# Projection weights on GpSimd's transfer queue, and four buffers for the last output tiles

## The chip, the cores and the metric

The kernel runs on one core of a Trainium2 chip. The metric is the device time of one execution in microseconds (us). TensorE (PE) does the matrix products, VectorE (DVE) and ScalarE (ACT) the elementwise work, GpSimd (POOL) a few small operations, and SyncE (SP) issues transfers.

## The reference

Two layers of a hybrid trunk, for 256 context and 512 latent tokens with 1024 channels, all in float32. In each layer one wide projection feeds three head groups, whose gated outputs are joined, projected back and added to the residual under a layer norm:

```python
h_l = x * (1 + sc_l) + sh_l
parts_l = jnp.split(h_l @ w_in, in_splits(), axis=-1)      # the same for the context, h_c
ssd_l, ssd_c = ssd_mixer(parts_c[0:3], parts_l[0:3], ...)
mla_l, mla_c = mla_mixer(parts_c[3:7], parts_l[3:7], ...)
ret_l, ret_c = retention_mixer(parts_c[7:11], parts_l[7:11], ...)
out_l = jnp.concatenate([ssd_l, mla_l, ret_l], -1) @ w_out
x_new = layer_norm(ALPHA * x + g_l * out_l, ln_g, ln_b)    # the result of layer 2 is the output
```

The modulations sh, sc and g of every layer come from products of a conditioning vector with `w_ada`.

## The kernel before, in words

**Tiling.** Activations lie channel-major, as tiles of 128 channels x 768 tokens (columns 0 to 255 context, 256 to 767 latent). Each weight matrix is cut into tiles of 128 partitions x 1024 columns (512 KB). A layer has 42 such tiles of `w_in` and 16 of `w_out`, so 116 in all.

**A weight tile's way** is `wslot` (L153). A transfer fills a raw buffer `wr` (two of them); ACT rounds it into `wh` (L122), and DVE takes the rest, `wl = wr - wh` (L124 through L104); `wh` and `wl` have three buffers each. A matrix product is then three passes (L145): high by high, high by low, low by high. A raw buffer is free again when `wl` has been made, and a `wh` when the products of the tile before it in that buffer are done. From the seventh tile on, `wslot` runs at high priority.

**Stages of a layer.** `dt_stage`, `xbc`, `ssd` and the spilled projections (the list STEPS, L48); `zstage` and `ret`; `mla_prep`; then `mla` with the first half of the output projection beside it (`out_s`, L1147, tiles `sh`, `sl`); and the second half with the layer norm (`out_m`, L1167, and `lns`, L1203, tiles `mr`, `mh`). Intermediate results are spilled to DRAM and loaded again, all through `load` (L97), which issues on SyncE's queue: `cf<-cum`, `kr<-kn`, `mraw<-m`, `la<-a` are such loads. Layer 1 of the trace ends near 850 us, where the first projections of the second layer (`proj_lat`, L194) begin.

**Order.** The kernel gives program order and priorities; the program builder makes from these, when the kernel is built, one fixed order of instructions per engine and per queue, and the waits between them. SyncE and GpSimd work their own lists off strictly in order: what waits holds up what is behind it.

**GpSimd's list** is short. It has the zeroing of `rh` in `ret` (L805), memsets of the attention's operand tiles in `mla` (L999 to L1002, tiles `bql`, `bkh`, `bkl`, `bvh`), the sums `lxs` over the first tiles in `lns` (L1232), and `rp_y`, a power of -0.5 of the variance in `rpow` (L142) that each layer norm needs before it can go on.

**The end.** `ln_turned` (L1265) writes the last 256 tokens token-major: it holds four accumulators `pot`, adds the mean's part to each by a product (L1289), scales each on DVE into a tile `ho` of 128 x 512 with two buffers (L1290, L1291), and stores it (L1292). Nothing comes after these stores.

Of the kernel before, what the change touches and what calls it, by code (L numbers as in the profile page):

```python
# [9 lines left out]
F32 = mybir.dt.float32  # L10
# [78 lines left out]
class Trunk:  # L89
# [63 lines left out]
    def wslot(self, src, n=1024):  # L153
        self.nslots += 1
        with (self.tc.high_priority() if self.nslots > 6 else ExitStack()):
            raw = self.wp.tile([128, 1024], F32, tag="wr", name="wr", bufs=2)
            self.load(raw[:, :n], src)
            hi = self.wp.tile([128, 1024], F32R, tag="wh", name="wh", bufs=3)
            lo = self.wp.tile([128, 1024], F32R, tag="wl", name="wl", bufs=3)
            self.split(hi[:, :n], lo[:, :n], raw[:, :n])  # L160
        return hi, lo
# [1103 lines left out]
    def ln_turned(self, P, X, a, b, qsum, xsum):  # L1265


        pc = self.pc[self.l]
        k = (b - a) // 128
        dg, lgr, lbr = self.turn  # L1270
        po = {}
        for f in range(2):
            for c in range(k):
                po[c, f] = (self.acc.tile([128, 512], F32, tag="acc", name="pot") if f or c else
                            self.ps("pot", "pot", 1))
                for t in range(4):
                    self.mm(po[c, f][:, t * 128:(t + 1) * 128], X[4 * f + t][:, c * 128:(c + 1) * 128], dg[:, 4 * f + t],
                            t == 0, False, skip_group_check=True)
        with self.tc.high_priority():
            pd = self.ps("plm", "pld", 2)  # L1280
            self.mm(pd[0:1, 0:b - a], self.selD[:, 0:1], xsum)
            nd = P.tile([1, 256], F32, name="nd")
            self.act(nd[:, 0:b - a], pd[0:1, 0:b - a], AF.Copy, scale=-1.0)
            v = self.variance(P, qsum, xsum, k)
            y = self.rpow(P, v, k)
        for f in range(2):
            fs = slice(512 * f, 512 * f + 512)
            for c in range(k):
                self.mm(po[c, f], nd[:, c * 128:(c + 1) * 128], lgr[:, fs], False, True, skip_group_check=True)  # L1289
                o = P.tile([128, 512], F32, tag="hr", name="ho", bufs=2)  # L1290
                self.stt(o, po[c, f], y[:, c:c + 1], lbr[:, fs], ALU.mult, ALU.add)  # L1291
                self.load(self.out[1][c * 128:(c + 1) * 128, fs], o)  # L1292

# [145 lines left out]
```

## Time and profile before

| | |
|---|---|
| median of 3 runs | 1485.49 us (1483.68 to 1488.11) |
| profiled execution, device time | 1483.76 us |
| its span, first to last instruction | 1481.8 us |
| TensorE busy | 1426.5 us, 96% of the span |
| VectorE, ScalarE, GpSimd busy | 73%, 47%, 2% |
| transfers | 226.18 MB, nearly all on one hardware queue |

The span leaves some 2.0 us of the device time around it. A busy TensorE in this profile is one with a product in its pipeline. A matrix product and the weight load for the next one overlap, so PE and PEld together are more than the span.

### The profile page before, as it was taken

What the parts mean: (1) busy time and instruction counts of PE and PEld (TensorE: products, weight loads), DVE (VectorE), ACT (ScalarE), POOL (GpSimd) and SP (SyncE); (2) the same over time, 40 slices, a digit from 0 to 9 for tenths busy, and PEclk for the clock granted to TensorE, in tenths of its full rate; (3) what the DMA queues carried; (4) which work ended last, traced back from release to release, by engine and by line L of the source; (5) the groups of instructions that cost most, each with busy time, mean ns of one, the idle gap of its engine ahead of it and who ended that gap; (6) DMA issues with size and microseconds to landing.
All of it is one profiled execution on the core that took longest, in us unless ns stands there. A gap on an engine that the chain in (4) does not pass through costs nothing. (4 is left out here: it accounts for less than half of the span.)

```text
span 1481.8 us, 23394 instructions
## 1 busy us (share of the span) xinstructions
PE 1426.5 (96%) x8696; PEld 1158.2 (78%) x8696; DVE 1076.6 (73%) x2077; ACT 692.6 (47%) x1377; POOL 25.7 (2%) x35
## 2 busy tenths in 40 slices
PE   6999999999999999999999899999999999989988
PEld 4787789778888888777788778788778887767667
DVE  3599894995486667678645858997776767678846
ACT  2346743662232443477622345565463344347742
POOL 0000000000000001000001000000000000100010
PEclk9999999999999999999999999999999999999999
DMA  8336553457725746624241223353357465562241
GB/s 337 138 99 180 183 168 110 158 184 256 258 72 175 247 154 198 222 82 131 80 170 58 91 88 111 120 148 114 98 168 251 136 199 190 171 205 89 69 141 57
DMA packets 109725, 226.18 MB, mean 153 GB/s; under 512 B 13534, under 2 KB 41310, under 8 KB 109356
## 3 DMA queue, kind: packets, MB, share of 16 engines
q1 hardware_dynamic: 109612, 224.70, 46.5%
q8 instruction: 68, 1.11, 0.3%
q14 instruction: 45, 0.37, 0.1%
HBM read 174.46 MB, written 50.20 MB: 152 GB/s over the span
## 5 line engine op out<-in xcount | busy, mean ns | idle before, releaser
L101 PE MATMUL pj<-hh,wh 128*128 128x512 f32 (+1 forms) x984 | 354.5, 361 | 2.8 <-ACT hh L115 2.4
L101 PE MATMUL pj<-hh,wl 128*128 128x512 f32 (+1 forms) x984 | 353.2, 359 | 0.0
L101 PE MATMUL pj<-hl,wh 128*128 128x512 f32 (+1 forms) x984 | 350.7, 356 | 0.0
L122 ACT CAST wh<-wr 128x1024 fp32r<-128x1024 f32 (+1 forms) x116 | 120.3, 1039 | 208.8 <-PE pj L101 92.2
L101 PEld LDWEIGHTS pj<-hh,wh 128*128 128x128 f32 x984 | 185.1, 188 | 36.0 <-issue 8.9
L101 PEld LDWEIGHTS pj<-hh,wl 128*128 128x128 f32 x984 | 185.0, 188 | 31.2 <-issue 7.0
L101 PEld LDWEIGHTS pj<-hl,wh 128*128 128x128 f32 x984 | 185.2, 188 | 30.5 <-issue 6.4
L104 DVE TENSOR_TENSOR wl<-wr,wh 128x1024 fp32r<-128x1024 f32 (+1 forms) x116 | 141.0, 1216 | 79.6 <-ACT wh L122 78.5
L104 DVE TENSOR_TENSOR pel<-pe,peh 128x512 fp32r<-128x512 f32 (+1 forms) x112 | 71.6, 648 | 37.0 <-ACT peh L115 36.5
L107 DVE SCALAR_TENSOR_TENSOR cv<-xpad,cw,cv 128x772 f32<-128x772 f32 (+1 forms) x96 | 92.2, 993 | 0.2
L115 ACT ACTIVATE pe<-psc 128x512 f32<-128x512 f32 (+1 forms) x112 | 63.7, 569 | 56.4 <-PE psc L101 47.6
L1043 DVE TENSOR_REDUCE nm<-pmx 128x1 fp32r<-128x768 f32 (+1 forms) x80 | 67.6, 845 | 15.7 <-PE pmx L101 14.5
L101 PE MATMUL po<-sh,wh 128*128 128x512 f32 (+1 forms) x192 | 70.0, 367 | 4.2 <-DVE oy L107 4.2
L101 PE MATMUL po<-sl,wh 128*128 128x512 f32 (+1 forms) x192 | 70.1, 366 | 1.9 <-DVE sl L107 1.9
L115 ACT ACTIVATE ce<-cf 64x512 f32<-64x512 f32 (+1 forms) x80 | 46.9, 587 | 50.3 <-DMA cf<-cum 49.5
L101 PE MATMUL po<-sh,wl 128*128 128x512 f32 (+1 forms) x192 | 69.6, 364 | 0.0
L115 ACT ACTIVATE tm<-sf,dt 128x128 f32<-128x128 f32 x160 | 52.5, 390 | 30.4 <-DVE sf L104 30.3
L115 ACT ACTIVATE peh<-psc 128x512 fp32r<-128x512 f32 (+1 forms) x112 | 63.6, 568 | 0.2
L101 PE MATMUL po<-mr,wh 128*128 128x256 f32 (+1 forms) x216 | 55.5, 343 | 3.1 <-DVE la L107 3.1
L115 ACT ACTIVATE arg<-arg,ncb 128x128 f32<-128x128 f32 x160 | 54.9, 393 | 4.1 <-DVE arg L107 3.6
L101 PE MATMUL pv<-wl,hh 128*128 128x256 f32 x192 | 54.0, 281 | 0.7 <-DVE wl L104 0.7
L101 PE MATMUL pv<-wh,hh 128*128 128x256 f32 x192 | 53.7, 280 | 0.0
(337 smaller groups left out, 2952.1 us busy)
## 6 DMA issues: line engine op xcount, KB each, us to landing
wr<-in_win SPq DMA_DIRECT2D x82, 512.0 KB, 3.8
ar<-in_wada SPq DMA_DIRECT2D x48, 512.0 KB, 7.0
cf<-cum SPq DMA_DIRECT2D x80, 256.0 KB, 4.6
wr<-in_wout SPq DMA_DIRECT2D x32, 512.0 KB, 4.3
y<-ys SPq DMA_DIRECT2D x20, 256.0 KB, 2.5
xs<-th SPq DMA_DIRECT2D x16, 256.0 KB, 2.1
x<-in_xT SPq DMA_DIRECT2D x8, 384.0 KB, 8.6
rv<-stv SPq DMA_DIRECT2D x24, 128.0 KB, 3.0
```

Source lines behind the costliest of these rows:

```text
L101: return self.nc.tensor.matmul(out, lhsT=lhsT, rhs=rhs, start=start, stop=stop, **k)
L104: return self.nc.vector.tensor_tensor(out, a, b, op=op)
L107: return self.nc.vector.scalar_tensor_tensor(out, in0=a, scalar=s, in1=b, op0=op0, op1=op1)
L115: return self.nc.scalar.activation(out, in_, f, **k)
L122: self.nc.scalar.copy(hi, raw)
L1043: nc.vector.tensor_reduce(nm[:, i:i + 1], p1[:, 0:n], axis=AX.X, op=ALU.max, negate=True)
```

## The change

From the fourth weight tile on, `wslot` issues its transfer from GpSimd's queue; the first three stay on SyncE's, as do all other transfers. The last output tiles `ho` get a tag of their own with four buffers in place of the two of tag `hr`.

```diff
@@ wslot
         self.nslots += 1
         with (self.tc.high_priority() if self.nslots > 6 else ExitStack()):
             raw = self.wp.tile([128, 1024], F32, tag="wr", name="wr", bufs=2)
-            self.load(raw[:, :n], src)
+            (self.nc.gpsimd if self.nslots > 3 else self.nc.sync).dma_start(out=raw[:, :n], in_=src)
             hi = self.wp.tile([128, 1024], F32R, tag="wh", name="wh", bufs=3)
@@ ln_turned
                 self.mm(po[c, f], nd[:, c * 128:(c + 1) * 128], lgr[:, fs], False, True, skip_group_check=True)
-                o = P.tile([128, 512], F32, tag="hr", name="ho", bufs=2)
+                o = P.tile([128, 512], F32, tag="ho", name="ho", bufs=4)
                 self.stt(o, po[c, f], y[:, c:c + 1], lbr[:, fs], ALU.mult, ALU.add)
                 self.load(self.out[1][c * 128:(c + 1) * 128, fs], o)
```

## Rows read from the trace of the kernel before

**Rows 1.** The page: busy us by engine; the chain that ended last, by engine.

```profile
PE 1426.5 (96%) x8696; PEld 1158.2 (78%) x8696; DVE 1076.6 (73%) x2077; ACT 692.6 (47%) x1377; POOL 25.7 (2%) x35
...
PE 31%; DVE 5%; DMA 3%; ACT 3%; issue 1%; SPq 0%; POOL 0%; DVEq 0%; ACTq 0%; POOLq 0%
```

**Rows 2.** Waits of PE: us in total, times, longest.

```profile
PE pr L101 <- DMA ar<-in_wada: 7.5, 2, 6.6
...
PE pv L101 <- DVE wl L104: 0.7, 1, 0.7
...
PE pj L101 <- ACT wh L122: 0.4, 1, 0.4
```

**Rows 3.** Tile wr: ns min/median/max; then what its users waited for (us, times).

```profile
L104 DVE TENSOR_TENSOR wl<-wr,wh x116: 551/1224/1487, 14.6 to 1449.3; 128x1024 fp32r<-128x1024 f32 x114, 128x384 fp32r<-128x384 f32 x2
L98 SPq DMA_DIRECT2D wr<-in_win x84: 327/333/1122, 4.5 to 1192.8; - x84
...
  PE pj L101: 92.2, 43
...
  DMA wr<-in_win: 3.7, 3
  DMA wr<-in_wout: 2.7, 1
...
DMA to landing us min/median/max: 3.2/3.9/9.2
```

**Rows 4.** Waits of SyncE's queue, the longest group.

```profile
SPq L98 <- DVE wl L104: 240.3, 67, 11.8
```

**Rows 5.** SyncE's timeline, 1293 to 1312: start, us, transfer.

```profile
1298.06 0.38 SPq L98 DMA_DIRECT2D qr<-qh  x1
1301.71 0.33 SPq L98 DMA_DIRECT2D wr<-in_wout  x1
1302.14 0.47 SPq L98 DMA_DIRECT2D kr<-kn  x1
```

**Rows 6.** PE's timeline in that stretch.

```profile
1303.27 0.79 PE L101 MATMUL po<-sh,wh 128*128 128x512 f32 x1 [3.69 <-DVE oy L107]
```

**Rows 7.** Windows: length, busy us of PE, PEld, DVE, ACT, POOL; granted clock; DMA share, GB/s.

```profile
592.70:629.80 37.10, 34.40 (x199) 26.69 (x198) 25.12 (x36) 18.27 (x33) 0.00 (x0) 0.91 0.67 222
815.00:852.00 37.00, 31.18 (x174) 26.65 (x173) 32.09 (x64) 12.37 (x19) 1.73 (x2) 0.91 0.25 91
1296.60:1333.60 37.00, 32.20 (x130) 23.44 (x129) 29.39 (x44) 17.29 (x28) 0.00 (x0) 0.91 0.68 205
```

**Rows 8.** DVE's timeline at the end, and SyncE's stores.

```profile
1474.28 1.54 DVE L107 SCALAR_TENSOR_TENSOR ho<-pot,rp_y,lbr 128x512 f32<-128x512 f32 x2 [1.08 <-PE pot L101]
1477.15 1.56 DVE L107 SCALAR_TENSOR_TENSOR ho<-pot,rp_y,lbr 128x512 f32<-128x512 f32 x2 [1.33 <-DMA out<-ho]
...
1475.06 4.01 SPq L98 DMA_DIRECT2D out<-ho  x4
```

**Rows 9.** POOL's timeline: start, us, operation, idle before.

```profile
794.76 0.74 POOL L1232 TENSOR_TENSOR lxs<-lxs,la 128x256 f32<-128x256 f32 x1 [1.18 <-DVE la L107]
829.83 1.03 POOL L142 TENSOR_TENSOR rp_y<-rvv,mhalf 128x4 f32<-128x4 f32 x1 [34.33 <-DVE rvv L104]
...
1293.60 0.74 POOL L1000 MEMSET bkh<- 1x768 f32 x1 [8.58 <-PE pq L101]
...
1443.16 2.28 POOL L1232 TENSOR_TENSOR lxs<-lxs,la 128x512 f32<-128x512 f32 x1 [0.90 <-DVE la L107]
```

**Rows 10.** SyncE's weight transfers at the end of the first layer.

```profile
796.61 8.97 SPq L98 DMA_DIRECT2D wr<-in_win  x2
...
829.27 0.33 SPq L98 DMA_DIRECT2D wr<-in_win  x1
...
831.85 0.33 SPq L98 DMA_DIRECT2D wr<-in_win  x1
```

**Rows 11.** PE's timeline there.

```profile
830.92 0.82 PE L101 MATMUL prs<-K,rp_y 128*128 128x128 f32 x5 [0.81 <-POOL rp_y L142]
```

**Rows 12.** DVE's timeline, a weight split beside POOL's sum.

```profile
786.75 1.49 DVE L104 TENSOR_TENSOR wl<-wr,wh 128x1024 fp32r<-128x1024 f32 x1 [0.48 <-ACT wh L122]
```

## The prediction

> **What bounds the kernel now.** I read the page's engine line first: TensorE is busy 96% of the span, so 1481.8 - 1426.5 = 55.3 us of idle time is nearly all that a better supply could win back [rows 1]. Then the waits of PE, to see who causes that idle time. The largest that names a transfer is 7.5 us at the very start, for the modulation weights, which the change leaves alone; waits for a weight tile's halves `wh` and `wl` come to 1.1 us over 116 tiles [rows 2]. The view of tile `wr` says why: its ACT and DVE users waited for a transfer four times, 6.4 us in all, but 92.2 us for products that still held a `wh` buffer [rows 3]. So weights wait for TensorE, not TensorE for weights. Last, SyncE's own waits: it stood 240.3 us, 67 times, at the head of its list for `wl`, that is, with a weight transfer whose raw buffer was not yet free [rows 4]. That is what the change removes from SyncE, and the question is who stood behind.
>
> **Weight transfers, moved.** 116 - 3 = 113 of them leave SyncE. Issuing one takes 0.33 us there [rows 3], 37 us in all, on a sequencer that is not on the chain of work (SPq 0%) [rows 1]: worth nothing by itself. On GpSimd no row shows what an issue costs. From below it is SyncE's 0.33 us [rows 3], from above the longest operation that GpSimd runs here, 2.28 us [rows 9]; I take 1.03 us, the time of `rp_y` with its four columns, since that is an instruction with hardly any data, as an issue is [rows 9]. The landing, 3.9 us at the median [rows 3], then comes some 0.7 us later (bounds 0 and 2). What hides this is that users of `wr` hardly ever wait for a transfer [rows 3]. Without that cover it would cost up to 113 x 0.7 = 79 us; with it I count 0.
>
> **What stood behind the weights on SyncE.** The clearest place is the start of the second layer's attention. SyncE ends `qr<-qh` at 1298.44, stands at a weight tile until 1301.71, and only then issues `kr<-kn` [rows 5], which the attention's operands need. On its own list `kr` could go 1302.14 - 1298.44 = 3.7 us earlier. TensorE stood 3.69 us in this stretch, but for `oy`, a DVE result of the output projection [rows 6]; the keys are not what it lacked. So bounds of 0 and 3.7 us gained; since the released wait is not the one that ended last, I take a value near the lower end, 0.5 us, for the room that earlier key splits leave on ACT and DVE.
>
> Here a page speaks against the change. In the rows, the queue's waiting costs little because other work covers it. The Trainium skill, in "DMA: Bandwidth & Descriptors", section "Issuing engines are not separate DMA queues", says that transfers from whichever engine run on the same 16 DMA engines and that several issuers save sequencer time only. By that rule this term would be 0 and the sum 0.5 us later. It doesn't speak of a sequencer that waits in order, which is what the SyncE rows show [rows 4, 5], so I keep the 0.5.
>
> **What the weights now stand among on GpSimd.** Its list is short, 35 instructions and 25.7 us [rows 1], but some are awaited. At the end of the first layer `rp_y` starts at 829.83, and TensorE stands 0.81 us for it before `prs` [rows 9, 11]. A weight transfer was issued at 829.27 and another at 831.85 [rows 10]. If the first keeps its place ahead of `rp_y`, GpSimd is busy with it until 829.27 + 1.03 = 830.30, and `rp_y` and TensorE come 0.47 us later. I count 0.47; the bounds are 0 (behind `rp_y`) and 3.05 (the second one also ahead: 831.85 + 1.03 - 829.83). The other way round, a weight may stand behind a memset: the one at 1293.60 waited 8.58 us for TensorE [rows 9]. A weight held for that long would mostly still land before a `wh` is free, by the 92.2 us that users spent waiting for TensorE [rows 3]; 0.
>
> **Beside VectorE.** The split of a weight tile took 1224 ns at the median and 1.49 us where GpSimd's sum `lxs` ran beside it [rows 3, 12]. If building a transfer's descriptors disturbs DVE as much, that is 113 x 0.27 = 30 us of DVE time, of which DVE's 5% of the chain [rows 1] would let 1.5 us through. I take 0, bounds 0 and 1.5.
>
> **Four output buffers.** At the end DVE makes two `ho`, waits 1.33 us for the first store to land, and makes two more; the stores are all that follows [rows 8]. With four buffers the second pair starts at 1474.28 + 1.54 = 1475.82 instead of 1477.15, if TensorE has finished all four accumulators by then, and the last store goes as much earlier. That is -1.33 us on the path itself (bounds -1.33 and 0).
>
> **Sum.** -1.33 + 0.47 - 0.5 = -1.4 us against the profiled execution's 1483.76: 1482.4. The median of the runs is 1.7 us above that execution, so the forecast in its terms is 1485.5 - 1.4 = **1484.1**. About 0.3%, 4.5 us, is what a measurement of this kernel can tell from no change: the forecast is no change.
>
> **Rivals.**
>
> *A: as summed.* 1484.1; with its bounds (0.47 up to 3.05, 1.5 for DVE, -0.5 down to -3.7) 1481 to 1488.
>
> *B: SyncE's freedom pays at the attention's starts.* The stretch 1296.6 to 1333.6 has 37.0 - 32.2 = 4.8 us idle, and a granted clock of 0.91, so (1 - 0.91) x 37 = 3.3 us lost to the lower of TensorE's two levels after that idle time; 592.7 to 629.8, the same stage of the first layer, has 2.7 and 3.3 us [rows 7]. If loads that come 3.7 us earlier let the builder put the key splits into ACT's and DVE's idle time ahead of the gap, the first 8.1 us can go: 1484.1 - 8.1 + 0.5 = 1476.5; half of it gives 1480.5. For it: SyncE's 240 us of waits are real [rows 4], and a change of queue lets the builder reorder neighbours everywhere. Against: TensorE's large wait there is for `oy` [rows 6].
>
> *C: GpSimd's list becomes the wait.* One mechanism: a weight transfer whose raw buffer isn't free stands at the head of GpSimd's list, and a sum or a power of the layer norm behind it. `lxs` of 794.76 behind the transfers from 796.61 on costs 796.61 + 1.03 - 794.76 = 2.9 us, `rp_y` behind that of 831.85 3.05 us [rows 9, 10]: 1485.5 - 1.33 + 5.9 = 1490.1, and 1493.4 if the longer gap costs another 3.3 us of clock as in the rows of that stretch [rows 7]. It decides from the point where one transfer ahead of `rp_y` still waits for a split. For it: the transfers fall within 2 us of both operations. Against: the builder would have to misjudge the order by about that much.
>
> *D: the buffers do nothing* because the last accumulators come later than 1475.8, and the rest cancels: 1485.5.
>
> **How the numbers follow.** A 0.40, B 0.36, C 0.19, D 0.05. A and D are no change, B is faster, C is slower; a little of B (half of its gain or less) stays within 0.3%, and a little of A's upper end goes beyond. Faster 0.35, same 0.45, slower 0.20. The range leaves out B's best and C's worst: 1475 to 1491.5; A's own range is 1481 to 1488.
>
> **What would show it.** Right: DVE's two pairs of `ho` follow each other without a gap; ACT and DVE still wait for `wr` transfers in only a few places; SyncE's wait for `wl` is gone, and TensorE's idle time stays near 55 us. B: `kr` is issued near 1298 and the idle time of that stretch falls from 4.8 to below 2 us. C: POOL's timeline shows `rp_y` or `lxs` right after a weight issue, and PE's wait for `rp_y` grows from 0.81 towards 3 us. The step most likely to be wrong is the 0 for the landings: if an issue on GpSimd takes far over 2.28 us, weights would be late everywhere, and the wait of PE for `wh` would show it. A new order of the other engines' work, which no row can show, is what would move the total most.

## The result, and the profile after

The changed kernel takes 1510.6 us (median of 4 runs) against 1484.6 beside it: a ratio of 1.0166, 95% interval 1.0146 to 1.0186. It is slower by some 25 us, on the other side of the forecast and outside its range. First the page of the changed kernel (its span, and busy time by engine), which answers to [rows 1]:

```profile
span 1506.4 us, 23467 instructions
...
PE 1436.0 (95%) x8696; PEld 1165.9 (77%) x8696; DVE 1077.9 (72%) x2077; ACT 691.3 (46%) x1377; POOL 86.3 (6%) x148
```

The span grew by 1506.4 - 1481.8 = 24.6 us. TensorE's idle time went from 55.3 to 70.4 us (+15.1), and the same 8696 products took 9.5 us more: a larger part ran at the lower clock (mean granted clock 0.977 against 0.987). Next, what the forecast worried about. The view of tile `wr`, which answers to [rows 3] (ns min/median/max of an operation; then one of those who waited for it, in us and times; then landings):

```profile
L104 DVE TENSOR_TENSOR wl<-wr,wh x116: 553/1225/1495, 14.6 to 1472.5; 128x1024 fp32r<-128x1024 f32 x114, 128x384 fp32r<-128x384 f32 x2
L158 POOL DMA_DIRECT2D wr<-in_win x81: 530/530/711, 18.1 to 1213.4; - x81
...
  ACT wh L122: 15.4, 5
...
DMA to landing us min/median/max: 3.3/4.1/9.9
```

An issue on GpSimd takes 0.53 us, a transfer lands in 4.1 us at the median instead of 3.9, and the split on VectorE takes 1225 ns as before. ScalarE's casts wait for these transfers five times, 15.4 us in all (four times and 6.4 us before); TensorE hardly feels it. TensorE's waits (us in total, times, longest), for [rows 2]:

```profile
PE pvv L101 <- ACT stv L115: 7.1, 2, 4.9
...
PE py L101 <- DVE tm L104: 3.3, 3, 1.7
PE pnm L101 <- DVE nm L1044: 3.3, 1, 3.3
...
PE pv L101 <- DVE wl L104: 0.4, 1, 0.4
PE pj L101 <- ACT wh L122: 0.4, 1, 0.4
```

Waits for weight halves are still 0.8 us in all. What grew are waits for results of ScalarE and VectorE other than weights. SyncE's wait for `wl`, 240.3 us in [rows 4], is gone (GpSimd's list has it now, 1101.0 us in 87 waits), and the queue waits for other things:

```profile
SPq L98 <- DVE th L107: 92.0, 11, 20.8
```

Where was the time lost? I cut both spans at the casts of the same weight tiles (the 22nd, 38th, 52nd, 94th and 109th) and read the view of windows (length, busy us of PE and the others, granted clock, DMA share, GB/s). Three stretches of the kernel before:

```profile
427.10:751.00 323.90, 317.18 (x1955) 257.21 (x1953) 222.67 (x400) 159.09 (x288) 5.16 (x8) 0.99 0.47 152
751.00:1144.50 393.50, 384.90 (x2235) 318.15 (x2235) 300.62 (x576) 174.11 (x363) 7.83 (x8) 0.99 0.40 129
1144.50:1299.40 154.90, 149.98 (x775) 122.47 (x773) 110.62 (x231) 56.92 (x83) 5.21 (x8) 0.99 0.56 183
```

And the same three of the changed kernel:

```profile
433.50:768.40 334.90, 322.40 (x1948) 261.05 (x1946) 223.17 (x398) 157.56 (x287) 12.46 (x22) 0.96 0.45 145
768.40:1161.90 393.50, 385.05 (x2240) 318.12 (x2240) 301.76 (x580) 173.71 (x362) 30.78 (x50) 0.99 0.42 136
1161.90:1324.30 162.40, 153.55 (x775) 125.31 (x775) 114.76 (x239) 57.94 (x85) 9.73 (x18) 0.96 0.50 161
```

The middle one, with 50 of GpSimd's instructions, costs nothing in this pair. The first costs 11.0 us and the third 7.5, with TensorE's clock down from 0.99 to 0.96; the two windows ahead of these cost 3.2 us each and the last one nothing. These are sizes, not exact prices: in single executions with the old order (e1, e3, e8 and e15 below) the first of the three is 1.0 to 4.5 us longer than in this one of before. Still, the loss isn't spread over the 113 transfers: it sits in certain stretches. Both programs hold the same instructions, and comparing them engine by engine shows what differs in these stretches: the order. The builder, which sorts each engine's instructions by its own plan of times, put 2456 of TensorE's 7487 instructions in other places, 672 of VectorE's 2071, 353 of ScalarE's 1376, and 216 of the 639 transfers on SyncE that carry no weight tile. GpSimd's own 35 kept theirs.

### The profile page after: what moved, and what is told of

Its sections match the earlier page's. It is cut to its first block, busy times and chain, and to the rows that moved or that the text cites. A ratio compares the mean times of both kernels' runs of the same rounds, so it can differ in the third digit from the quotient of the medians.

```text
span 1506.4 us, 23467 instructions
## 1 busy us (share of the span) xinstructions
PE 1436.0 (95%) x8696; PEld 1165.9 (77%) x8696; DVE 1077.9 (72%) x2077; ACT 691.3 (46%) x1377; POOL 86.3 (6%) x148
## 5 line engine op out<-in xcount | busy, mean ns | idle before, releaser
L158 POOL DMA_DIRECT2D wr<-in_win x81 | 43.5, 537 | 831.3 <-DVE wl L104 587.0
L101 PE MATMUL pv<-wh,hl 128*128 128x256 f32 x192 | 54.5, 284 | 0.0
```

The source lines that it names most:

```text
L101: return self.nc.tensor.matmul(out, lhsT=lhsT, rhs=rhs, start=start, stop=stop, **k)
L158: (self.nc.gpsimd if self.nslots > 3 else self.nc.sync).dma_start(out=raw[:, :n], in_=src)
```

## Experiments

**Holding an order.** To separate the queue from the order, an order has to be carried from one kernel to another. The edit below, put behind the kernel's body, adds an order-only edge from each instruction of an engine to the next in a list taken from the other kernel's built program. Weight transfers and GpSimd's own instructions aren't in the lists; the builder places these. In the traces the four engines run in the sequence that they were held to.

```diff
+ORDER = {'PE': '...', 'DVE': '...', 'Activation': '...', 'SP': '...'}
+
+def hold(tc):
+    have = {i.name: i for i in tc.nc.cur_bb.bb.instructions}
+    info = mybir.DependencyInfo(mybir.DependencyClass.NoSync, mybir.DependencyReason.DATA)
+    for text in ORDER.values():
...
+        for a, b in zip(row, row[1:]):
+            tc.add_manual_dep(b, a.name, info, reason="order")
 def body(tc, A, out):
     Trunk(tc, A, out).run()
+    hold(tc)
```

**e1: the change, in the order of before.** The changed kernel with `hold` and the lists of the kernel before.

> The changed kernel (weights from GpSimd's queue, four buffers), but TensorE, VectorE, ScalarE and SyncE are held to the exact order of instructions that they had in the kernel before. Theory O (the 25 us come from the new order that the builder gave the engines when the loads changed queue, not from the loads): the time falls back to about 1484, between 1479 and 1489; what is left is the cost or gain that the prediction priced, -0.8 us with its bounds. Theory S (the loads themselves cost more on GpSimd's software path: later landings, its issues on the port, rp_y behind them): it stays near 1510, 1505 to 1513. Theory F (SyncE, freed of its waits, issues the other transfers earlier and they collide): its order is the same but it can still run ahead, so most of the loss stays, 1500 or more.

Measured: 1.0017 (0.9998 to 1.0035), 1488.5 us. The 25 us are gone, with all 113 transfers still on GpSimd. Theories S and F fall as causes of the 25 us.

**e2: the order without the change.** The kernel before with `hold` and the lists of the changed kernel.

> The kernel before (weights from SyncE's queue, two buffers), but the four engines are held to the order that they have in the changed kernel; only the places of the weight loads in SyncE's list are the builder's. Theory O: slow without any change of queue, 1506 to 1514. Theory S and theory F: nothing that they blame is in this kernel, so about 1485 (1481 to 1490). Near 1495 would say that both halves count.

Measured: 1.0278 (1.0247 to 1.0309), 1527.4 us. The new order alone is slow; it is even 17 us slower than the changed kernel, which no theory had. I come back to this with e11.

**e3 and e4: one half of the change each.**

```diff
-                o = P.tile([128, 512], F32, tag="hr", name="ho", bufs=2)
+                o = P.tile([128, 512], F32, tag="ho", name="ho", bufs=4)
```

> Only the four final output buffers; queues and order as before. The prediction's term for them is -1.33 us: 1483 to 1484, inside what can be told from no change. All theories of the 25 us put none of it here; if the placement of the buffers mattered it would be above 1490.

> Only the change of queue, with the two old buffers. All theories that blame the queue or the order it brings: 1509 to 1513, the changed kernel's time and at most 2 us more. If the buffers have a share in the loss it falls below 1505.

Measured: e3 0.9998 (0.9981 to 1.0014), e4 1.0162 (1.0132 to 1.0192). In the traces e3 has the order of before on every engine, and e4 that of the changed kernel. The buffers have no share in the loss.

**e5 and e6: the order of one stretch.** As e1, but with the changed kernel's order between the 38th and the 51st weight cast; and the reverse.

> As the run with the order of before (weights from GpSimd's queue, four buffers), but from the cast of the 38th weight tile to that of the 51st (427 to 709 us of the trace of before: the end of layer 0's projections, its output products and the start of its attention) the four engines have the order of the changed kernel. Between these casts the changed kernel fell behind by 11 us more (from 6.5 to 17.4 us). Theory L (the loss is made stretch by stretch, by the order in it): 1488 + 11, 1496 to 1502. Theory C (the loss is a cascade: an early order sets what comes late for the rest): either near 1488, since the early part is as before, or near 1510.

> The complement: the changed kernel with its own order, but with the order of before in that one stretch. Theory L: 1511 - 11, 1497 to 1503. Theory C: still near 1510, since the order of the early part, which it blames, is the new one, or near 1488.

Measured: e5 1.0095 (1.0069 to 1.0122), e6 1.0070 (1.0045 to 1.0094). e5 is 0.78% above e1, 11.6 us for the 11 expected (which are counted to the 52nd cast, as in the windows above); e6 is 0.96%, 14 us, below the changed kernel, each to within some 5 us. The traces put it in the stretch itself: from the 38th to the 52nd cast e5 takes 11.8 us longer than e1, and e6 11.2 us less than the changed kernel. Both say theory L: a stretch costs what the order in it costs. And it can be read there. Near 600 us TensorE stands 0.2 us for `nm` in e1. Here are SyncE's transfers in e1 (start, us, transfer):

```profile
597.67 0.32 SPq L98 DMA_DIRECT2D a<-ox  x1
598.03 4.20 SPq L98 DMA_DIRECT2D mraw<-m  x3
602.27 0.46 SPq L98 DMA_DIRECT2D kr<-kn  x1
602.77 0.58 SPq L98 DMA_DIRECT2D kr<-krr  x1
603.40 0.43 SPq L98 DMA_DIRECT2D gt<-g  x1
```

The same transfers in the changed kernel:

```profile
613.54 0.46 SPq L98 DMA_DIRECT2D kr<-kn  x1
614.05 0.58 SPq L98 DMA_DIRECT2D kr<-krr  x1
614.68 0.41 SPq L98 DMA_DIRECT2D gt<-g  x1
616.26 0.34 SPq L98 DMA_DIRECT2D a<-ox  x1
616.64 6.59 SPq L98 DMA_DIRECT2D mraw<-m  x3
```

The three gate and key loads went from behind `mraw` to ahead of it, and so did a weight transfer, which in e1 follows at 599.07. Here are that transfer, the casts of `mraw` on ScalarE, the split on VectorE and TensorE's product in the changed kernel:

```profile
615.66 0.53 POOL L158 DMA_DIRECT2D wr<-in_wout  x1 [10.26 <-DVE wl L104]
```

```profile
623.69 1.78 ACT L122 CAST mr<-mraw 128x768 fp32r<-128x768 f32 x2 [9.33 <-DMA mraw<-m]
```

```profile
624.55 0.96 DVE L104 TENSOR_TENSOR mr<-mraw,mr 128x768 fp32r<-128x768 f32 x1 [2.79 <-ACT mr L122]
625.43 0.95 DVE L1044 TENSOR_REDUCE nm<-pmx 128x1 fp32r<-128x768 f32 x1
```

```profile
626.43 0.37 PE L101 MATMUL pnm<-identr,nm 128*1 128x128 f32 x2 [3.29 <-DVE nm L1044]
```

Read them from below: TensorE waits 3.29 us for `nm`; `nm` was delayed by nothing of its own but stands on VectorE behind the split `mr`, which waits 2.79 us for the cast of an `mraw`; and the cast waited for that transfer. SyncE had issued it at 616.64 without a wait, but it landed only at 623.6, 7.0 us later. In e1 the one of 598.03 landed in 3.5 us, at 601.5:

```profile
601.56 0.83 ACT L122 CAST mr<-mraw 128x768 fp32r<-128x768 f32 x1 [3.14 <-DMA mraw<-m]
```

That it lands late because of the transfers put ahead of it fits the two lists, but no run isolates them. What the order decides is shown by e5, with the new order in that stretch only: its weight transfer goes out ahead of `mraw` too, `mraw` takes 7.0 us, ScalarE's cast waits 9.54 us for it, and TensorE stands as in the changed kernel:

```profile
PE pnm L101 <- DVE nm L1044: 3.3, 1, 3.3
```

A second place is that of the first output products. Before, the query products `pq` stand between the last gate projection and the first `po`, and cover the 9 us that ScalarE and VectorE need to make `sh` and `sl` from it. In the changed kernel all `pq` of that part come first, and TensorE has nothing left when the projection ends. Its first output products there:

```profile
575.72 0.50 PE L101 MATMUL po<-sh,wh 128*128 128x512 f32 x1 [1.11 <-ACT sh L115]
...
577.74 0.77 PE L101 MATMUL po<-sh,wh 128*128 128x512 f32 x1 [1.15 <-DVE mod L112]
578.57 0.79 PE L101 MATMUL po<-sl,wh 128*128 128x512 f32 x1
```

The gaps are 2.3 us, but the products behind them take 0.63 to 0.79 us instead of 0.40 for 10 us: the granted clock is 1.00 from 565 to 576 us, 0.52 from 577 to 587, and 0.97 in the 10 us after, that is 2.4 GHz, then 1.2, then 2.4 again. In such places 15 us of idle time become 25 us of span.

The wait that grew most, 4.9 us for `stv` at 1279 us, lies in the third stretch. ScalarE, which makes `stv`, stands 6.40 us there for the landing of a store `v<-stv`. SyncE issued it behind `a<-ox`; before and in e1 two such stores go out ahead of `a<-ox`. No run isolates that place.

**e7 and e8: another queue, and a single transfer.**

```diff
-            self.load(raw[:, :n], src)
+            (self.nc.scalar if self.nslots > 3 else self.nc.sync).dma_start(out=raw[:, :n], in_=src)
```

> The kernel before with the weights from the fourth tile on issued from ScalarE's queue, two buffers, order left to the builder, which makes a third order of it (half of TensorE's places differ from both). If any order other than the tuned one costs (the order of before is a good draw among many): 1495 to 1530. If the software queue were what makes a kernel slow: near 1485, since ScalarE's transfers are of the hardware kind. ScalarE's own waits for free slots come in front of its casts, so some of a loss could be its own, seen as waits of ScalarE's queue.

> The kernel before, but one weight transfer alone (the 20th, near 230 us) comes from GpSimd's queue; the order of every engine stays that of before. In the changed kernel GpSimd's last drain lasted 10.05 us from its last instruction, against 0.80 before, and SyncE's last drain waited for it some 1.4 us at the end. If that drain is the price of having used the queue at all: 10 us again and the end 1.4 us later after the last store than before (4.6 against 3.1 us). If it stems from transfers that are still under way or from the number of them: 0.8 us as before.

e7 measured 0.9938 (0.9916 to 0.9959), faster than both kernels: my expectation that any order but the tuned one costs was wrong. An order is a draw, and this third one is better. e8 (one run, 1486.6 us against 1487.5, which decides nothing on the time) showed a drain of 0.90 us, so the price isn't paid for using the queue at all; more under the hardware below.

**e9, e10 and e11: queue and order crossed.** Old order on ScalarE's queue; the third order on GpSimd's and on SyncE's.

> Weights from ScalarE's queue as in the run that gained 0.6%, but the four engines held to the order of before. Theory O (the order alone makes the gain, as it made the loss): the gain goes, ratio 0.998 to 1.003, as GpSimd's queue with the order of before had 1.0017. Theory Q (ScalarE's queue itself pays): the ratio stays near 0.994.

> The changed kernel (weights from GpSimd's queue, four buffers), held to the order that the builder made for ScalarE's queue. Theory O: the same edit that cost 1.7% now gains, 1479 to 1483 where before has 1486, a ratio of 0.994 to 0.998 (1.4 us of GpSimd's drain at the end included). Theory S (GpSimd's loads cost under any order): 1.002 or more.

> The kernel before, weights from SyncE's queue, held to the same third order. Theory O in its pure form: the order does not care for the queue, 0.994. Rival W (an order made for a queue of its own needs one: on SyncE's the loads that wait for a slot hold up other transfers, as in the run with the changed kernel's order on SyncE's queue, which was 17 us slower than the changed kernel itself): 1.000 to 1.012, with waits of PE on transfers of other tiles.

Measured: 1.0025 (1.0012 to 1.0038), 1.0008 (0.9988 to 1.0029) and 1.0172 (1.0154 to 1.0189). As a table of ratios:

| order | weights from SyncE | from GpSimd | from ScalarE |
|---|---|---|---|
| of the kernel before | 1 | 1.0017 (e1) | 1.0025 (e9) |
| made for GpSimd's queue | 1.0278 (e2) | 1.0166 (the change) | not run |
| made for ScalarE's queue | 1.0172 (e11) | 1.0008 (e10) | 0.9938 (e7) |

Theory O holds down the columns: in GpSimd's, with the same transfers on the same queue, the order alone moves the time by 1.5 to 1.6%. But it is not the whole: in its pure form it fails in the last row, and rival W is right there in kind, though e11 lies above its 1.000 to 1.012. e11's trace shows one place. SyncE's list (first fence), and what VectorE and TensorE then waited for:

```profile
1159.54 2.07 SPq L98 DMA_DIRECT2D wr<-in_win  x2
1161.66 0.43 SPq L98 DMA_DIRECT2D g<-st  x1
1162.14 1.89 SPq L98 DMA_DIRECT2D rgt<-rg  x4
...
1165.95 5.42 SPq L98 DMA_DIRECT2D zx<-xs  x3
```

```profile
1170.26 0.75 DVE L107 SCALAR_TENSOR_TENSOR zy<-zx,pc,zy 128x512 f32<-128x512 f32 x1 [9.02 <-DMA zx<-xs]
...
1171.53 0.68 DVE L104 TENSOR_TENSOR kd<-pkt,te 128x512 f32<-128x512 f32 x1
```

```profile
1172.26 2.08 PE L101 MATMUL prst<-rvt,kd 128*128 128x128 f32 x8 [6.98 <-DVE kd L104]
```

Two weight loads, each waiting for a split, stand ahead of `g`, `rgt` and `zx`; SyncE issued nothing between 1153.8 and 1159.5 us. VectorE then waits 9.02 us for `zx`, and `kd` behind it makes TensorE wait 6.98 us. In e7, where the weights are on ScalarE's queue, the first `zx` goes out 3.8 us after the 93rd weight cast; here it is 13.2 us. So the wait that the change was seen to remove does cost, in an order that hasn't been arranged around it: 7 us in this place, of the 2.3% between e11 and e7; the rest is not traced. In the order of before it costs nothing (e1, e9).

e10's whole interval lies above the 0.994 to 0.998 that theory O expected. Under this order GpSimd's queue does cost some 0.6% against ScalarE's, which theory O doesn't have (e12 below, with the same four buffers, is at 0.9947). The profiled span of e10 is 6.7 us above e7's: 1.5 us from the last `rp_y` to the end, where the drain is, and the rest mostly lower clock (mean 0.983 against 0.988). Why the same order loses more clock with GpSimd's queue stays open.

**e12: e7 with four buffers.**

> ScalarE's queue with its own order, and the four final buffers. From the start of the last rp_y to the end of the span the kernel before needed 9.31 us, the one with four buffers alone 8.97: so 0.3 us less than with two, ratio 0.993 to 0.995, which no timing tells from the run with two; in the profile the last two products of the tail, not a store, should end the wait of VectorE.

Measured 0.9947 (0.9930 to 0.9964), 1478.0 us, which the time doesn't tell from e7. VectorE's four last tiles follow each other without a gap here:

```profile
1469.25 3.26 DVE L107 SCALAR_TENSOR_TENSOR ho<-pot,rp_y,lbr 128x512 f32<-128x512 f32 x4 [1.09 <-PE pot L101]
```

From `rp_y` to the end it needs 8.14 us and e7, with two buffers, 9.28: a gain of 1.14, not the expected 0.3. In e3 the same edit had gained 0.34, since VectorE waited for TensorE's `pot` instead:

```profile
1481.41 0.75 DVE L107 SCALAR_TENSOR_TENSOR ho<-pot,rp_y,lbr 128x512 f32<-128x512 f32 x1 [0.95 <-PE pot L101]
```

In e3 the clock falls to its lower level at 1479 us, under TensorE's last products for `pot`, which end at 1481.4; in e12 it falls at 1472.0, when they are done (1471.7).

**e13 and e14: whose order?** The changed kernel with TensorE alone held to the order of before, and with the other three held.

> The changed kernel with TensorE alone held to its order of before; the builder then places the instructions of VectorE, ScalarE and SyncE anew (778, 382 and 227 of them stand elsewhere than before). If the loss lies in TensorE's own order (products whose operands are late put ahead of ready ones): 1484 to 1491. If it lies in the order of the engines that feed it: TensorE waits for late operands in the old order too, 1500 or more.

> The complement: VectorE, ScalarE and SyncE held to the order of before, TensorE left to the builder, which then differs from before in 724 of 7487 places, none of them before the 2588th. If TensorE's order carries the loss: above 1495, if these 724 places hold a good part of it. If the feeding engines' order carries it: 1484 to 1491.

Measured: e13 1.0232 (1.0207 to 1.0257), e14 1.0038 (1.0023 to 1.0052), 1491.5 us, just above the 1484 to 1491 expected. Both speak for the order of the engines that feed TensorE: an old order on TensorE, fed in a new one, is worse than the change itself, and with the old order of the feeders the builder places TensorE's products almost as well as before. They do not prove it, since the engines left free got an order of their own: by the traces, VectorE's in e13 differs from the changed kernel's in 630 of 2071 places, and TensorE's in e14 in 2190 of 8696.

**e15: the second layer alone.** The kernel before with `nslots > 58` in place of 3.

> The kernel before with only the second layer's 58 weight transfers on GpSimd's queue, two buffers, order free: the builder changes nothing in the first layer (TensorE's first 4492 places are as before). Theory L: only what the second layer's new order costs, 0 to 8 us (the changed kernel lost 3.6 us net there): 1485 to 1494. The last drain, 0.90 us after one transfer and 10.05 after 113, would be 5 to 6 us if it grows with their number, and then ends before SyncE's and costs nothing.

Measured: 1.0011 (0.9995 to 1.0028). With the first layer's order kept, most of the loss is gone. At the 58th weight cast the changed kernel is 19.7 us behind the profiled execution of before. This one is 5.8 behind, with the same order as before up to that point, so by the spread of single executions. The drain took 5.56 us and cost nothing.

## Why the prediction was wrong

**The step that failed** is the one without a term. The prediction closed with "a new order of the other engines' work, which no row can show, is what would move the total most", and then gave it neither a price nor a chance. It stood only in rival B, as something that "lets the builder reorder neighbours" for a gain. Measured, that step is +22 us (1.0166 against e1's 1.0017), and on the other side. A range that held it would have had to be about twice as wide: the orders tried here, each free on its own queue, run from 0.9938 to 1.0166, 34 us where the range has 16.5. That a new order would come could be known, since the builder plans all engines together and 113 transfers on another queue change its plan; its size no row of before had.

**The sum itself** was worked out from rows of the old order, and e1 is the change in that order: -1.4 us forecast; measured +2.5 us, between -0.3 and +5.2, so the sum is outside by a little. Term by term:

- *Issue and landing, 0.* Right. 0.53 us against the 1.03 taken; the landing at the median is 3.9 us in e1 as before, and 4.1 in the changed kernel; waits of TensorE for `wh` and `wl` are 1.2 us in e1 and 0.8 in the changed kernel, against 1.1.
- *SyncE freed, -0.5.* In the order of before it gives 0 where the prediction looked. In e1 `kr<-kn` goes out at 1299.84 instead of 1302.14 [rows 5], and TensorE's idle time in that stretch is 37.00 - 32.08 = 4.9 us where it was 4.8 [rows 7]. Rival B's mechanism did not happen. The Trainium skill, in "DMA: Bandwidth & Descriptors", section "Issuing engines are not separate DMA queues", says that several issuers save sequencer time only, by which the term was 0. e1 and e9 agree with it (1.0017 and 1.0025). e11 against e7 does not: there the separate queue is worth 2.3%, in part by the waits in the list, of which the section doesn't speak.
- *`rp_y` behind a weight issue, +0.47.* Right in kind, small in size. In e1 (and alike in the changed kernel) the issue stands directly ahead of it, and TensorE's wait goes from 0.81 [rows 11] to 1.6. `rp_y` starts 0.47 us later than its operand would let it, as forecast, which is luck: the issue is half as long as taken and starts later. Besides, `rp_y` runs 0.24 us longer than before, for a reason that no run shows:

```profile
831.45 0.54 POOL L158 DMA_DIRECT2D wr<-in_win  x1 [23.69 <-issue]
832.00 1.27 POOL L142 TENSOR_TENSOR rp_y<-rvv,mhalf 128x4 f32<-128x4 f32 x1
```

```profile
PE prs L101 <- POOL rp_y L142: 1.6, 1, 1.6
```

  Rival C's mechanism is there and costs nothing more: the transfer ahead of `rp_y` did stand 23.69 us at the head of GpSimd's list, for the split that freed its buffer, but that split ended at 830.9, half a us before the operand of `rp_y` was ready (831.4). The one that would have been late, at 833.81, the builder placed behind. In the changed kernel TensorE's wait is 0.5 us.
- *VectorE beside GpSimd, 0.* Right: 1225 ns against 1224 [rows 3].
- *Four buffers, -1.33.* The mechanism is right, with the condition that the prediction named ("if TensorE has finished"). It is met at full clock (-1.14 in e12) and not at the lower one (-0.34 in e3). In the changed kernel too the last `ho` waits for TensorE:

```profile
1497.41 2.40 DVE L107 SCALAR_TENSOR_TENSOR ho<-pot,rp_y,lbr 128x512 f32<-128x512 f32 x3 [1.08 <-PE pot L101]
1500.75 0.75 DVE L107 SCALAR_TENSOR_TENSOR ho<-pot,rp_y,lbr 128x512 f32<-128x512 f32 x1 [0.94 <-PE pot L101]
```

- *GpSimd's last drain, not in the sum.* About +1.4 us at the end (last section).

With +0.8 at `rp_y`, -0.1 for the buffers in e1 (from the last `rp_y` to VectorE's last product 6.13 us against 6.22) and +1.4 for the drain, the terms as measured come to +2.1 us, beside the +2.5.

Rival D was closer than the forecast for the buffers, but none of the rivals had the loss.

**Still open:** why the builder's plan for GpSimd's queue comes out worse than those for the others. The runs show what its order does on the chip, not what the plan took into account.

## What to carry to other kernels

Where a builder sorts the instructions, a change of queue is also a new order of every engine, and the order can weigh far more than the edit itself, 22 us against 2.5 here: compare the programs' orders first, and time the edit once with the old order held to learn what the edit itself is worth. In a forecast, price the new order by its own spread, on both sides. Here the wait at the head of SyncE's list was worth nothing while the order had work around it, and up to 2.3% where it hadn't; so removing it paid only along with an order made for it, and that on ScalarE's queue alone.

## What was not expected of the hardware

GpSimd's last drain, which starts with its last instruction, grows with the number of transfers that it has issued (nearly all of 512 KB, so number and bytes are not told apart). From the trace's records:

| kernel | transfers from GpSimd | last drain, us |
|---|---|---|
| before | 0 | 0.80 |
| e8 | 1 | 0.90 |
| e15 | 58 | 5.56 |
| the change, e1, e10 | 113 | 10.05 |

This is 0.82 + 0.0817 x n within 0.02 us for the last three. The last instruction is the final `rp_y`, 9.3 us ahead of the end in the kernel before, so with 58 transfers the drain is hidden, and with 113 it is what the end waits for: in e1 SyncE's last drain is done at 1480.7 us, and GpSimd answers at 1482.1.

By the same records a weight transfer starts 0.03 us (median) after the split that frees its raw buffer when SyncE issues it (before) or ScalarE (e7), and 0.29 us after it when GpSimd does (the change).
